# Attention's first tiles over the recurrence's scratch, and the first squares added by VectorE, in a fused FoX / RWKV-7 / memory-attention layer

## The chip, the cores and the metric

The kernel runs on one core of a Trainium2 chip. The metric is the device time of one execution in microseconds; the time of a kernel is the median of its runs.

## The reference

One inference step of one layer, for a prompt of 2048 tokens (width 1024) and for 8 decoding sequences of 16 tokens each, which go through the same projection as 128 further rows. All arithmetic is float32. Cut to what matters here:

```python
h = rms_norm(x, norm_g) @ w_in                        # 1024 -> 3654 columns
fox_cols, rwkv_cols, mem_cols = split(h)
q, k, v, logf, g_f = fox_prep(fox_cols, ...)          # QK-norm, log forget gates
o_f = softmax(q k^T / 8 + c_q - c_k, causal) @ v      # 6 heads x 64, c = cumsum(logf)
xs  = token_shift(rwkv_cols, prev, mu)
o_r, s_new, g_r = rwkv_branch(xs, s0, ...)            # 6 heads x 64, delta-rule state scan
o_m = mem_attend(mq, mk, mv)                          # 4 heads x 64 into 256 memory tokens
o = concat(o_f * silu(g_f), o_r * silu(g_r), o_m * silu(g_m))
y = x + o @ w_out
# rms_norm(x, g) = x * rsqrt(mean(x * x) + eps) * g
```

Outputs are `y` for prompt and samples, the new keys, values and log forgets, the memory's keys and values, the recurrence's last states and the last projected rows.

## The kernel before, in words

Precision is kept by splitting each float32 operand into a high part and the rest (`S.copy` to a rounded type on ScalarE, then a subtraction on VectorE or GpSimd), and by three matmuls: high x high, high x low, low x high. All matmuls go through the helper `mm` (line 59), elementwise operations of two tensors through `tt` (62), with a scalar through `stt` (65) and `ts` (68). So one line of the profile holds many uses, and tiles tell them apart.

**Phase 1** (`p1`) walks over the tokens in four rounds of 512, the first with the 128 sample rows added (640). A round begins with `prep_x`: squares of x, their sums over the 1024 features, `rsqrt` of the mean, x times that norm, split into `xk` (eight tiles). In the first round x comes transposed (features on the partitions), in two groups of 256 and 384 tokens; the squares (`xsq`, line 251, ScalarE) are summed over features by matmuls with a column of ones into `pq`, 128 tokens at a time, one matmul for each feature tile and each 128 tokens. `rsqrt_small` (a scale and add on VectorE, a power on GpSimd) gives `rsq`; a matmul with the identity spreads it (`pb`), and ScalarE copies it to `rb` (269). Later rounds square on ScalarE with an accumulator (261). Then come the LoRA columns (`lora_in`), the columns of the recurrence (`shifted`, `rwkv_in`, `rwkv_mid`, `rwkv_scan`, `rwkv_out`) and the other columns (`wide`, `pair`), as filler between the stages of the recurrence. Projections accumulate in the PSUM tiles `pjd` and `pjt` (pool `pj`). The last round ends with the memory's keys and values (`memory_x`, split tiles `xm` over the recurrence's scratch) and the last states, transposed into `pst` and copied out (937 to 940).

**Phase 2** (`p2`) is attention and the output projection. A unit is a pair of heads and a block of 512 queries. `turned_in` loads tokens into `tok` and transposes them into the PSUM tile `pt`; `split_keys` makes `K1` and `K2`, `queries` makes `Q1` and `Q2`; `fox_max` computes logits (`pm`) and their row maxima on VectorE; `negate` and `rows_` put the negated maxima into `Q1` as an extra row; `attend` computes scores (`pS`), exponentials (`P`, split into `Ph` and `Pl`) and values (`po`), which are copied to `ob`. Memory attention, the samples and the output projection (`out_weights`, `project`, PSUM tile `py` with the tag `pt`) are mixed in between as filler. Weights are loaded as `wr`, split into `W`. `cl` (976 to 983) is the running sum of the samples' cached log forgets.

Memory is handed out by pools, each a stretch of SBUF or PSUM that lies behind the pools opened before it. When phase 1's pools close, phase 2's pools are laid over them, and a tile of phase 2 must wait until all tiles of the phase 1 pools under its pool are done. Before, the order in phase 1 is `c1, rv, sm, rw, xs, ws` in SBUF (constants and state; recurrence tiles; small tiles; recurrence scratch; x; weights) and `pj, pg, ps` in PSUM (3, 2 and 3 banks). In phase 2 it is `lt, c2, kp, wk` in SBUF, which puts `c2` and `kp` over `xs`, and `wk` over `ws`; and `qa` (`pt`, 3 banks), `qb` (`pm`, 2), `qc` (`pS` and `po`, 3) in PSUM, which puts `qa` over `pj` and `qc` over `ps`.

The order of all instructions is not that of the code. `_arrange` collects the whole program, gives every instruction an estimated cost, and runs a list scheduler (`_schedule`) over both phases: on each engine the instruction that can start earliest goes first, ties broken by a rank (`_Problem.emitted`: its place in the program in TensorE's time, less a share of the work that hangs on it). It runs 18 times, with ranks moved between runs towards the middle of the earliest and latest start, and takes the order with the shortest estimate. The order is fixed in the program; each engine, and SyncE's queue of DMA issues, runs its list strictly in that order. What the scheduler knows of overlapping pools is worked out from the tiles' sizes (`_overlaps`).

Of the kernel before, what the change touches and what calls it, by code (L numbers as in the profile page):

```python
# [16 lines left out]
D = 1024  # L17
# [8 lines left out]
PL = "G"  # L26
FILL = 0
WRAW, WHL = 2, 4
# [23 lines left out]
def kernel(ctx: ExitStack, tc: tile.TileContext, I: dict, O: dict):  # L52
# [70 lines left out]
    with ExitStack() as p1:  # L123
        c1 = pools(p1, "c1")

        def c1t(name, shape, dtype=F32):
            return c1.tile(shape, dtype, tag=name, name=name)

        maskG = c1t("maskG", [128, 2, 128], BF16)
        reset = c1t("reset", [128, 640], BF16)  # L130
        bones = c1t("bones", [128, 128], F32R)
# [6 lines left out]
        for dst, src, s1, s2 in ((HW0, V_W0, 0.5, 0.0), (HA0, V_A0, 0.5, 0.0), (NKK, V_KK, -1.0, 0.0),  # L138
                                 (HKK, V_KK, 0.5, 0.0), (HKA, V_KA, 0.5, 0.0), (OHKA, V_KA, -0.5, 1.0),
                                 (GW5, V_GNW, 0.5, 0.0), (GB5, V_GNB, 0.5, 0.0)):  # L140
            ts(V, vh[:, dst:dst + 3], vec[:, src:src + 3], s1, s2, M, A_)
        WUP = c1t("WUP", [96, 2, 384], F32R)
        shp = c1t("shp", [128, 13, 8])
# [4 lines left out]
        V.memset(carry, 0.0)  # L148
        LW = c1t("LW", [96, 2, 640], F32R)
        ST = c1t("ST", [128, 3, 64])  # L150
        V.memset(ST, 0.0)
        AR0 = [c1t(f"AR0_{j}", [128, 2, 512]) for j in range(2)]
        WX = [c1t(f"WX_{j}", [128, 8 * 65]) for j in range(1)]
        XT = [c1t(f"XT_{j}", [128, 8, 64]) for j in range(2)]
        for j in range(2):
# [8 lines left out]

        rv = pools(p1, "rv")
        sm = pools(p1, "sm", bufs=2)
        rw = pools(p1, "rw")
        xs_ = pools(p1, "xs")
        ws = pools(p1, "ws", bufs=WHL)
        pj = pools(p1, "pj", bufs=3, space=bass.MemoryType.PSUM)  # L170
# [51 lines left out]
        def prep_x(tok0, n, xtok, xT, gcol, tiles=None, between=lambda: None):  # L222
# [9 lines left out]
            for t0, t1 in ((0, 2), (2, 5)) if first else ((0, nt),):  # L232
                c0, c1 = 128 * t0, 128 * t1
                if first:
# [14 lines left out]
                    for k in range(KC):  # L249
                        sq = sqs[k // 5 if t0 else 0][:, k % 5 if t0 else k, :]  # L250
                        S.activation(sq, raws[k][:, c0:c1], AF.Square)
                        for t in range(t1 - t0):
                            mm(pq[:, t:t + 1], sq[:, 128 * t:128 * t + 128], one1, start=k + t == 0, stop=k == KC - 1)
                    rsqrt_small(rsq[:, t0:t1], pq[:, 0:t1 - t0], t1 - t0, 1.0 / D, EPS)
# [688 lines left out]
    with ExitStack() as p2:  # L943
        lt = pools(p2, "lt", bufs=2)
        fill = lt.tile([128, FILL], BF16, tag="fill", name="fill", bufs=1) if FILL else None
        c2 = pools(p2, "c2")

        def c2t(name, shape, dtype=F32):
            return c2.tile(shape, dtype, tag=name, name=name)

        kp = pools(p2, "kp")
        wk = pools(p2, "wk", bufs=2)
        qa = pools(p2, "qa", bufs=PTB, space=bass.MemoryType.PSUM)
        qb_ = pools(p2, "qb", bufs=PMB, space=bass.MemoryType.PSUM)
        qc = pools(p2, "qc", space=bass.MemoryType.PSUM)

# [17 lines left out]

        cl = lt.tile([48, 512], F32, tag="P", name="cl", bufs=PB)
        SY.dma_start(cl, I["clf"])
        one48 = lt.tile([48, 512], F32, tag="P", name="one48", bufs=PB)
        V.memset(one48, 1.0)
# [38 lines left out]
        def fox_keys(U, hp):  # L1017

            cs = slice(128 * hp, 128 * hp + 128)
            U["K1"], U["K2"], U["vt"] = [], [], []  # L1020

            def block(g0):
                gs = slice(g0, g0 + 512)
                pt = turned_in(k_d[gs, cs], 512)
                k1 = [kp.tile([128, 512], F32R, tag="K1", name="K1", bufs=2 * NKB) for _ in range(2)]
                k2 = [kp.tile([128, 512], F32R, tag="K2", name="K2", bufs=2 * NKB) for _ in range(2)]
                for h in range(2):
                    split_keys(k1[h], k2[h], pt[64 * h:64 * h + 64], 512)
# [24 lines left out]
        def queries(U, q, qsrc, qb, hp, fox):  # L1053
# [23 lines left out]
            def fox_max(h, t, c0, nk):  # L1077
                n = min(512, nk - c0)
                pm = qb_.tile([128, 512], F32, tag="pm", name="pm", bufs=PMB)
                mm(pm[:, :n], q["Q1"][h][:, 128 * t:128 * t + 128], U["K1"][c0 // 512][h][:, :n])  # L1080
                to = q["mx"][:, h, t, c0 // 512:c0 // 512 + 1]
                if c0 + n == nk:

                    V.tensor_tensor_reduce(out=pm[:, :n], in0=pm[:, :n], in1=mneg[:, 512 - n:], scale=1.0,
                                           scalar=-3.0e38, op0=A_, op1=MAX, accum_out=to)
                else:
                    V.tensor_reduce(out=to, in_=pm[:, :n], op=MAX, axis=AX.X)  # L1087
# [39 lines left out]
        def attend(U, q, qb, hp, fox, gsrc, dst):  # L1127
# [6 lines left out]
            def scores(kt, h):  # L1134
# [5 lines left out]
                if fox and kt >= 4 * qb:  # L1140
                    tt(V, pS[:, c0:c0 + 128], pS[:, c0:c0 + 128], negm[:, 2, :], A_)
                P_ = lt.tile([128, 512], F32, tag="P", name="P", bufs=PB)
                S.activation(P_[:, c0:], pS[:, c0:], AF.Exp, bias=NB[:, qb, 2 * hp + h, kt:kt + 1] if fox else 0.0)  # L1143
                Ph = lt.tile([128, 512], F32R, tag="Ph", name="Ph", bufs=HB)
                Pl = lt.tile([128, 512], F32R, tag="Pl", name="Pl", bufs=LB)
                S.copy(Ph[:, c0:], P_[:, c0:])  # L1146
# [3 lines left out]
            def values(kt, h):  # L1150
# [8 lines left out]
                if kt == last - 1:  # L1159
# [3 lines left out]
                    if h:  # L1163
                        rs = lt.tile([1, 512], F32, tag="rs", name="rs", bufs=1)
                        S.copy(rs, po[h][64:65])
                        S.copy(R["ob"][64:128], po[h][0:64])  # L1166
                    else:

                        S.copy(R["ob"][0:65], po[h][0:65])
                        rs = R["ob"][64:65]  # L1170
# [153 lines left out]
        def out_weights(ks):  # L1324
            W = {}

            def load(k):
                raw = lt.tile([128, D], F32, tag="xo", name="wr")
# [7 lines left out]
        def project(W, ks, t, xsrc, dst):  # L1336
# [3 lines left out]
            def load():  # L1340
                ot = lt.tile([128, 5, 128], F32, tag="ot", name="ot", bufs=1)[:, :n]
                for a, k in enumerate(ks):
                    if a == 0 or k != ks[a - 1] + 1:
                        m = next((b for b in range(a + 1, n) if ks[b] != ks[b - 1] + 1), n) - a
                        SY.dma_start(ot[:, a:a + m], o_d[128 * k:128 * (k + m), ts_].rearrange("(k p) t -> p k t", p=128))
                W["x", t] = xt = lt.tile([128, D], F32, tag="xo", name="xo")
                SY.dma_start(xt, xsrc[ts_, :])
# [133 lines left out]
_TRIES = ((0.3, 0), (0.45, 0), (0.6, 0))  # L1481
_AGAIN = 6
_SHIFT = 0.4
_LOOSE = ("pt", "pj")
# [246 lines left out]
class _Problem:  # L1731
# [306 lines left out]
```

## Time and profile before

| | |
|---|---|
| median of 3 runs | 1809.12 us (1807.52 to 1819.66) |
| profiled execution, its own time | 1797.65 us |
| its span, first to last instruction | 1795.9 us |
| mean granted TensorE clock | 0.972 |
| TensorE busy | 1696.7 us (94%) |
| VectorE, ScalarE, GpSimd busy | 978.1, 897.9, 811.8 us |
| DMA | 303.11 MB, mean 169 GB/s |

The rows of the profile are one execution. A row of the view in order of time has start, length (both in us), engine, line, operation, output and inputs, shape, how many instructions are merged in it, and in brackets how long the engine stood idle before it and what released it. PE is TensorE, DVE VectorE, ACT ScalarE, POOL GpSimd, SPq SyncE's queue of DMA issues. A row of a tile's view has the count, the shortest, median and longest duration in ns, and the first and last start. One float32 matmul shows as two records.

### The profile page before, as it was taken

How to read it: one execution, taken by the hardware profiler on the slowest of the kernel's cores; microseconds unless marked ns; L12 is line 12 of the kernel's file. 1: busy time of each engine (PE TensorE's matmuls, PEld its weight loads, DVE VectorE, ACT ScalarE, POOL GpSimd, SP SyncE). 2: the span in 40 equal slices, each digit the busy share in tenths (PEclk: the TensorE clock that was granted, in tenths of full speed). 3: DMA queues.
4: the chain of work that ended last, by engine and by line, in shares of the span. 5: the costliest groups of instructions: out<-in, count | busy, mean ns of one | idle time of the engine just before them, and what ended most of it. 6: DMA issues, size and time to landing. Idle time of an engine off the chain costs nothing.

```text
span 1795.9 us, 41000 instructions
## 1 busy us (share of the span) xinstructions
PE 1696.7 (94%) x16313; PEld 1362.8 (76%) x16313; DVE 978.1 (54%) x2295; ACT 897.9 (50%) x1783; POOL 811.8 (45%) x824
## 2 busy tenths in 40 slices
PE   7989999999999999999899999799999899999998
PEld 6989989687887788886688887466667666667776
DVE  4654655572454564354574372776745765675214
ACT  5424343523243524233324343588898778886552
POOL 3654543242322242131132151477788566866552
PEclk8999999999999999999999999799999999999999
DMA  6763846653644654644635654534445772444432
GB/s 196 267 202 117 269 144 206 209 178 120 212 156 142 244 184 159 198 155 140 204 109 168 195 160 132 166 121 154 128 149 169 251 251 89 138 142 157 154 111 106
DMA packets 236314, 303.11 MB, mean 169 GB/s; under 512 B 81594, under 2 KB 185976, under 8 KB 220250
## 3 DMA queue, kind: packets, MB, share of 16 engines
q1 hardware_dynamic: 236122, 300.49, 51.5%
q8 instruction: 128, 2.10, 0.5%
q14 instruction: 64, 0.52, 0.1%
HBM read 210.15 MB, written 90.28 MB: 167 GB/s over the span
## 4 chain that ended last, share of the span: by engine, by line
PE 37%; DMA 7%; DVE 7%; ACT 7%; issue 2%; POOL 2%; SPq 1%; DVEq 0%; POOLq 0%; ACTq 0%
PE py L59 8%; PE po L59 6%; PE pjd L59 6%; PE pS L59 5%; PE pjt L59 3%; PE pm L59 2%; ACT P L1143 1%; DMA inv_d<-yt 1%; ACT Ph L1146 1%; POOL Pl L62 1%; DMA sp_d<-spr 1%; DMA xd<-inv_d 1%; DMA rb<-rd 1%; PE pz L59 1%; PE sc L59 1%
## 5 line engine op out<-in xcount | busy, mean ns | idle before, releaser
L59 PE MATMUL pjd<-xk,w 128*128 128x512 f32 (+4 forms) x2280 | 540.2, 378 | 13.0 <-ACT xk L279 4.6
L59 PEld LDWEIGHTS pjd<-xk,w 128*128 128x128 f32 (+1 forms) x2280 | 386.5, 192 | 80.8 <-issue 10.5
L62 POOL TENSOR_TENSOR Pl<-P,Ph 128x512 fp32r<-128x512 f32 (+3 forms) x272 | 318.8, 1183 | 160.6 <-ACT Ph L1146 132.8
L59 PE MATMUL pjt<-w,xk 128*128 128x256 f32 x2040 | 291.4, 290 | 3.9 <-issue 3.9
L59 PEld LDWEIGHTS pjt<-w,xk 128*128 128x128 f32 x2040 | 265.6, 192 | 10.1 <-issue 4.1
L59 PE MATMUL py<-W,oh 128*128 128x512 f32 x816 | 242.6, 399 | 0.9 <-ACT W L1331 0.4
L1143 ACT ACTIVATE P<-pS,NB 128x512 f32<-128x512 f32 x240 | 147.5, 624 | 87.1 <-PE pS L59 34.4
L59 PEld LDWEIGHTS py<-W,oh 128*128 128x128 f32 x816 | 150.9, 189 | 40.1 <-issue 1.0
L59 PE MATMUL pS<-Q,K 128*128 128x512 f32 x480 | 156.6, 387 | 7.1 <-ACT P L1143 4.7
L1146 ACT CAST Ph<-P 128x512 fp32r<-128x512 f32 (+3 forms) x272 | 150.7, 564 | 11.0 <-PE po L59 6.2
L59 PE MATMUL po<-Ph,vt 128*65 128x512 f32 x480 | 153.5, 371 | 2.6 <-ACT ob L1166 1.7
L59 PEld LDWEIGHTS pS<-Q,K 128*128 128x128 f32 x480 | 86.0, 193 | 45.4 <-ACT P L1143 21.6
L1087 DVE TENSOR_REDUCE mx<-pm 128x1 f32<-128x512 f32 x144 | 95.7, 685 | 25.1 <-PE pm L59 23.7
L62 POOL TENSOR_TENSOR nr<-nr,mhalf 128x8 f32<-128x8 f32 (+2 forms) x43 | 62.3, 1448 | 100.3 <-DVE nr L68 87.7
L62 POOL TENSOR_TENSOR w<-wraw,w 128x1024 fp32r<-128x1024 f32 (+1 forms) x34 | 81.6, 2411 | 46.2 <-ACT w L201 33.4
L59 PE MATMUL pm<-K,Q 128*128 128x512 f32 (+2 forms) x240 | 91.2, 399 | 9.2 <-DVE mx L1087 4.0
L59 PE MATMUL po<-Pl,vt 128*65 128x512 f32 x240 | 88.3, 369 | 3.1 <-POOL Pl L62 2.9
L62 DVE TENSOR_TENSOR xo<-py,xo 128x512 f32<-128x512 f32 x68 | 46.2, 685 | 77.9 <-PE py L59 77.6
L59 PEld LDWEIGHTS po<-Ph,vt 128*65 128x65 f32 x480 | 63.4, 136 | 30.9 <-ACT ob L1166 3.3
L62 DVE TENSOR_TENSOR ytmp<-yt 64x14 f32<-64x14 f32 (+9 forms) x210 | 55.0, 262 | 41.8 <-DMA yt<-ld 37.1
L718 ACT COPY qk<-pjt 128x512 f32<-128x512 f32 (+1 forms) x47 | 26.1, 564 | 97.0 <-PE pjt L59 96.7
L59 PEld LDWEIGHTS pm<-K,Q 128*128 128x128 f32 x240 | 46.1, 195 | 31.8 <-DVE mx L1087 11.3
(401 smaller groups left out, 2843.8 us busy)
## 6 DMA issues: line engine op xcount, KB each, us to landing
w<-w_d SPq DMA_DIRECT2D x84, 1024.0 KB
w_d<-w SPq DMA_DIRECT2D x28, 1024.0 KB
y_d<-xo SPq DMA_DIRECT2D x21, 512.0 KB
wraw<-in_w_in SPq DMA_DIRECT2D x36, 256.0 KB
xo<-in_x SPq DMA_DIRECT2D x17, 512.0 KB
xo<-y_d SPq DMA_DIRECT2D x17, 512.0 KB
xt<-in_x SPq DMA_DIRECT2D x24, 256.0 KB
xraw<-in_xT SPq DMA_DIRECT2D x24, 256.0 KB
```

The source lines that it names most:

```text
L59: PE.matmul(out, lhsT, rhs, start=start, stop=stop, skip_group_check=True)
L62: e.tensor_tensor(out=out, in0=a, in1=b, op=op)
L718: S.copy(o_, out)
L1087: V.tensor_reduce(out=to, in_=pm[:, :n], op=MAX, axis=AX.X)
L1143: S.activation(P_[:, c0:], pS[:, c0:], AF.Exp, bias=NB[:, qb, 2 * hp + h, kt:kt + 1] if fox else 0.0)
L1146: S.copy(Ph[:, c0:], P_[:, c0:])
```

## The change

It has four parts.

1. In SBUF, phase 1's order becomes `c1, rv, sm, ce, rw, xs, ws`, where the new pool `ce` takes from `c1` the tiles that only the recurrence's inputs use. In phase 2 `lt` gives five kinds of tile to a new pool `lp`, the first key block of the first pair of heads gets a pool of its own, `k0`, and the order becomes `lt, c2, wk, k0, kp, lp`. A tile `gap` fills `lt` up. `cl` and its ones take the two buffers of `ob`.
2. In PSUM, phase 2's order becomes `qc, qb, qa`. The maxima of the first unit use `pt` tiles.
3. The first 120 nodes of the schedule, counted from the first that uses `c2`, start with a rank that is 60 us earlier.
4. In the first round VectorE adds the eight tiles of squares into the first, and one matmul for each 128 tokens sums over the partitions.

```diff
-FILL = 0
...
     with ExitStack() as p1:
         c1 = pools(p1, "c1")
+        rv = pools(p1, "rv")
+        sm = pools(p1, "sm", bufs=2)
+        ce = pools(p1, "ce")
+        rw = pools(p1, "rw")
+        xs_ = pools(p1, "xs")
+        ws = pools(p1, "ws", bufs=WHL)
...
-        reset = c1t("reset", [128, 640], BF16)
+        reset = c1t("reset", [128, 640], BF16, ce)
-        WUP = c1t("WUP", [96, 2, 384], F32R)
+        WUP = c1t("WUP", [96, 2, 384], F32R, ce)
-        LW = c1t("LW", [96, 2, 640], F32R)
+        LW = c1t("LW", [96, 2, 640], F32R, ce)
-        AR0 = [c1t(f"AR0_{j}", [128, 2, 512]) for j in range(2)]
-        WX = [c1t(f"WX_{j}", [128, 8 * 65]) for j in range(1)]
-        XT = [c1t(f"XT_{j}", [128, 8, 64]) for j in range(2)]
+        AR0 = [c1t(f"AR0_{j}", [128, 2, 512], F32, ce) for j in range(2)]
+        WX = [c1t(f"WX_{j}", [128, 8 * 65], F32, ce) for j in range(1)]
+        XT = [c1t(f"XT_{j}", [128, 8, 64], F32, ce) for j in range(2)]
...
                         S.activation(sq, raws[k][:, c0:c1], AF.Square)
-                        for t in range(t1 - t0):
-                            mm(pq[:, t:t + 1], sq[:, 128 * t:128 * t + 128], one1, start=k + t == 0, stop=k == KC - 1)
+                        if k:
+                            tt(V, sqs[0][:, 0, :], sqs[0][:, 0, :], sq, A_)
+                    for t in range(t1 - t0):
+                        mm(pq[:, t:t + 1], sqs[0][:, 0, 128 * t:128 * t + 128], one1, start=t == 0)
...
         lt = pools(p2, "lt", bufs=2)
         c2 = pools(p2, "c2")
+        wk = pools(p2, "wk", bufs=2)
+        k0 = pools(p2, "k0", bufs=2)
         kp = pools(p2, "kp")
-        wk = pools(p2, "wk", bufs=2)
+        lp = pools(p2, "lp", bufs=2)
+        qc = pools(p2, "qc", space=bass.MemoryType.PSUM)
+        qb_ = pools(p2, "qb", bufs=PMB, space=bass.MemoryType.PSUM)
         qa = pools(p2, "qa", bufs=PTB, space=bass.MemoryType.PSUM)
-        qb_ = pools(p2, "qb", bufs=PMB, space=bass.MemoryType.PSUM)
-        qc = pools(p2, "qc", space=bass.MemoryType.PSUM)
+        gap = lt.tile([128, 112], F32, tag="gap", name="gap", bufs=1)
+        V.memset(gap[0:1, 0:1], 0.0)
...
-        cl = lt.tile([48, 512], F32, tag="P", name="cl", bufs=PB)
+        cl = lt.tile([48, 512], F32, tag="ob", name="cl")
-        one48 = lt.tile([48, 512], F32, tag="P", name="one48", bufs=PB)
+        one48 = lt.tile([48, 512], F32, tag="ob", name="one48")
...
-                k1 = [kp.tile([128, 512], F32R, tag="K1", name="K1", bufs=2 * NKB) for _ in range(2)]
-                k2 = [kp.tile([128, 512], F32R, tag="K2", name="K2", bufs=2 * NKB) for _ in range(2)]
+                at, more = (kp, {"bufs": 2 * NKB}) if hp or g0 else (k0, {})
+                k1 = [at.tile([128, 512], F32R, tag="K1", name="K1", **more) for _ in range(2)]
+                k2 = [at.tile([128, 512], F32R, tag="K2", name="K2", **more) for _ in range(2)]
...
-                pm = qb_.tile([128, 512], F32, tag="pm", name="pm", bufs=PMB)
+                pm = (qb_.tile([128, 512], F32, tag="pm", name="pm", bufs=PMB) if hp or qb else
+                      qa.tile([128, 512], F32, tag="pt", bufs=PTB, name="pm"))
...
# P, Ph, Pl, rs and the raw tiles "xo" (wr, xo): lt.tile(...) becomes lp.tile(...)
...
+_FIRST, _AHEAD = 120, 60000
...
+        first = min(x for x in range(self.count) for n in self.used[x] if self.pool[n].startswith("c2"))
+        for x in range(first, first + _FIRST):
+            rank[x] -= _AHEAD
         return rank
```

More of the change, by code (lines that the diff above doesn't have):

```diff
@@ L124, with c1t @@
         c1 = pools(p1, "c1")
-        def c1t(name, shape, dtype=F32):
-            return c1.tile(shape, dtype, tag=name, name=name)
+        rv = pools(p1, "rv")
[4 more added lines that the diff above has]
+        ws = pools(p1, "ws", bufs=WHL)
+        def c1t(name, shape, dtype=F32, pool=c1):
+            return pool.tile(shape, dtype, tag=name, name=name)
         maskG = c1t("maskG", [128, 2, 128], BF16)
-        reset = c1t("reset", [128, 640], BF16)
+        reset = c1t("reset", [128, 640], BF16, ce)
         bones = c1t("bones", [128, 128], F32R)
@@ L163 @@
         first16 = c1t("first16", [128, 1])
[L165 to L169, printed above, removed]
         pj = pools(p1, "pj", bufs=3, space=bass.MemoryType.PSUM)
@@ L944 @@
         lt = pools(p2, "lt", bufs=2)
-        fill = lt.tile([128, FILL], BF16, tag="fill", name="fill", bufs=1) if FILL else None
         c2 = pools(p2, "c2")
@@ L1141, in scores @@
                     tt(V, pS[:, c0:c0 + 128], pS[:, c0:c0 + 128], negm[:, 2, :], A_)
-                P_ = lt.tile([128, 512], F32, tag="P", name="P", bufs=PB)
+                P_ = lp.tile([128, 512], F32, tag="P", name="P", bufs=PB)
                 S.activation(P_[:, c0:], pS[:, c0:], AF.Exp, bias=NB[:, qb, 2 * hp + h, kt:kt + 1] if fox else 0.0)
-                Ph = lt.tile([128, 512], F32R, tag="Ph", name="Ph", bufs=HB)
-                Pl = lt.tile([128, 512], F32R, tag="Pl", name="Pl", bufs=LB)
+                Ph = lp.tile([128, 512], F32R, tag="Ph", name="Ph", bufs=HB)
+                Pl = lp.tile([128, 512], F32R, tag="Pl", name="Pl", bufs=LB)
                 S.copy(Ph[:, c0:], P_[:, c0:])
@@ L1163, in values @@
                     if h:
-                        rs = lt.tile([1, 512], F32, tag="rs", name="rs", bufs=1)
+                        rs = lp.tile([1, 512], F32, tag="rs", name="rs", bufs=1)
                         S.copy(rs, po[h][64:65])
@@ L1327, in load @@
             def load(k):
-                raw = lt.tile([128, D], F32, tag="xo", name="wr")
+                raw = lp.tile([128, D], F32, tag="xo", name="wr")
                 SY.dma_start(raw, I["w_out"][128 * k:128 * k + 128, :])
@@ L1345, in load @@
                         SY.dma_start(ot[:, a:a + m], o_d[128 * k:128 * (k + m), ts_].rearrange("(k p) t -> p k t", p=128))
-                W["x", t] = xt = lt.tile([128, D], F32, tag="xo", name="xo")
+                W["x", t] = xt = lp.tile([128, D], F32, tag="xo", name="xo")
                 SY.dma_start(xt, xsrc[ts_, :])
```

## The prediction, made before the change was run

> **What bounds the kernel now.** I read the page's busy shares and slices first, to see which engine is full and where it is not.
>
> ```profile
> PE 1696.7 (94%) x16313; PEld 1362.8 (76%) x16313; DVE 978.1 (54%) x2295; ACT 897.9 (50%) x1783; POOL 811.8 (45%) x824
> ```
> ```profile
> PE   7989999999999999999899999799999899999998
> ```
>
> TensorE (PE) is busy 94% of the span. Each slice is 44.9 us, and only two of them fall to 7: slice 0, the start, and slice 25 (1122 to 1167 us), where phase 1 (projections and recurrence) gives way to phase 2 (attention). So I cut the span into stages around both; the columns are the stage, its length, busy time of PE, its weight loads, VectorE (DVE), ScalarE (ACT) and GpSimd (POOL) with counts, granted clock, DMA share and GB/s.
>
> ```profile
> 12.00:24.70 12.70, 11.65 (x53) 11.36 (x54) 8.84 (x24) 6.15 (x18) 5.68 (x7) 1.00 0.66 185
> 24.70:41.00 16.30, 10.11 (x46) 7.94 (x46) 9.55 (x23) 11.20 (x28) 4.54 (x4) 0.79 0.56 183
> 41.00:60.00 19.00, 16.49 (x91) 15.17 (x91) 13.61 (x21) 9.94 (x23) 13.19 (x12) 0.82 0.90 300
> 60.00:1120.00 1060.00, 1013.64 (x12622) 866.25 (x12621) 550.74 (x1366) 381.59 (x809) 350.93 (x354) 0.98 0.54 176
> 1120.00:1130.00 10.00, 10.00 (x89) 7.22 (x87) 1.58 (x5) 3.25 (x7) 1.88 (x2) 1.00 0.14 45
> 1130.00:1138.00 8.00, 4.07 (x19) 3.04 (x17) 5.63 (x11) 1.64 (x4) 5.30 (x9) 0.92 0.56 171
> 1138.00:1160.00 22.00, 16.39 (x48) 10.43 (x49) 18.01 (x44) 15.24 (x27) 6.72 (x13) 0.50 0.67 207
> 1160.00:1175.00 15.00, 12.04 (x49) 7.75 (x48) 14.87 (x36) 12.33 (x27) 11.28 (x15) 0.86 0.41 137
> ```
>
> From 60 to 1120 us PE is busy 1013.64 of 1060 (95.6%) at a clock of 0.98: little to win, and the change does not touch it. At the hand-over, busy time times clock gives PE's work at full speed: 4.07 x 0.92 + 16.39 x 0.50 + 12.04 x 0.86 = 22.3 us in the 45 us from 1130 to 1175. So **22.7 us are lost there**, the most that half of the change could win. In those 45 us VectorE is busy 5.63 + 18.01 + 14.87 = 38.5: it is nearly full while PE is not. Just before, from 1120 to 1130, VectorE has 1.58 of 10 us and the DMA share is 0.14: room that nothing uses.
>
> PE's own rows, in order of time, say what it stood for.
>
> ```profile
> 1129.95 4.13 PE L59 MATMUL pjd<-xk,w 128*128 128x512 f32 x17
> 1138.08 1.11 PE L1004 MATMUL pt<-ident,tok 128*128 128x128 f32 x4 [4.00 <-DVE gth L65]
> ```
> ```profile
> 1159.64 1.11 PE L59 MATMUL po<-Ph,vt 128*65 128x512 f32 x2
> ```
>
> The last projection ends at 1134.08. The first attention transpose (`pt`) starts at 1138.08, released by the VectorE read of the last gate projection: that read empties the `pj` banks, and `pt` lies over them. From there it takes 21.6 us to the first values matmul (`po`).
>
> **The change, part by part.** *PSUM.* `pt` moves from the banks of `pj` to those of `ps`. The last user of `ps` is the transposed final state, copied here:
>
> ```profile
> 1130.40 0.46 ACT L939 COPY sstp<-pst 64x384 f32<-64x384 f32 x1
> ```
>
> So `pt` may start at 1130.86 instead of 1138.08: **7.2 us earlier**, beside the last 3.2 us of projections. The scores and `po` banks move over `pj`, which that same read frees at about 1138.0. They are first needed when keys and queries are split (below: eight casts of 0.58 on ScalarE, 4.6 us), so not before 1135.5, and the maxima follow first. I count this as hidden; if scores wait for it, up to 2 us come back.
>
> *SBUF.* Adding up the tiles' sizes, pool by pool, the constants and loaded tokens (`c2`) and queries (`wk`) now lie over the recurrence's scratch `ce` and `rw`, the first keys (`k0`) over `rw`, instead of over the projection's inputs, which live until 1134.08.
>
> ```profile
> 1112.91 0.69 DVE L62 TENSOR_TENSOR ya<-pa,AR 128x512 f32<-128x512 f32 x1 [2.67 <-PE pa L59]
> ```
> ```profile
> 1117.48 0.72 PE L59 MATMUL pjt<-w,xm 128*128 128x256 f32 x4
> ```
> ```profile
> 1134.11 0.37 SPq L1001 DMA_DIRECT2D tok<-k_d  x1
> ```
>
> `ce` is read last at 1113.6 and `rw` (which holds the memory's `xm`) at 1118.2, so the loads that now issue at 1134.11 can go 16 to 20 us sooner, into the quiet stretch. By themselves they are worth nothing, as `pt` waits longer for its banks; without them the earlier banks would be worth nothing either. The key and query parts follow from 1131: for each of the two, four casts on ScalarE and two subtractions on VectorE, priced by these rows. The bias table `NB` on VectorE (1.32 + 3 x 0.24 = 2.0 us) can leave the crowded stretch altogether.
>
> ```profile
> 1139.23 0.58 ACT L993 CAST K<-pt 64x512 fp32r<-64x512 f32 x1 [0.49 <-PE pt L1004]
> ```
> ```profile
> 1140.32 0.69 DVE L62 TENSOR_TENSOR K<-pt,K 64x512 fp32r<-64x512 f32 x1 [0.86 <-ACT K L994]
> ```
> ```profile
> L62 DVE TENSOR_TENSOR NB<-nck,off x4: 244/245/1322, 1134.5 to 1137.9; 128x96 f32<-128x96 f32 x4
> ```
>
> How much of the 7.2 us survives? What follows is VectorE's: it idles 45 - 38.5 = 6.5 us from 1130 to 1175, and 2.0 of its work can leave, so the ramp cannot end more than about 8.5 us sooner unless work is put off. Floor: if phase 1's own tail (gates, group norm) holds VectorE, about 2. I take **8** for the hand-over: the row nearest is the 7.2, and the output weights' raw tiles, which move to space free at 1134, add a little. Moving `cl` and its ones into the two `ob` buffers delays nothing while the copy-out of `po` comes after the write of `cl`; both are rows of this trace:
>
> ```profile
> L983 SPq DMA_DIRECT2D np_d<-cl x1: 320/320/320, 1156.5 to 1156.5; - x1
> ```
> ```profile
> L1169 ACT COPY ob<-po x2: 572/577/582, 1170.1 to 1190.6; 65x512 f32<-65x512 f32 x2
> ```
>
> 13.6 us of room; at 8 us earlier, 5.6 remain. That cover gone, each us of it is a us of PE. First maxima through three `pt` banks instead of two `pm` banks: nothing to 1 us, and I take nothing, VectorE being their limit.
>
> *First squares.* Now 40 matmuls with one output column sum the squares; then VectorE adds the eight tiles (14 additions in all) and 5 matmuls remain.
>
> ```profile
> 4.57 6.98 PE L59 MATMUL pq<-one,xsq 128*128 128x1 f32 x32 [4.57 <-ACT xsq L251]
> 12.59 1.22 PE L59 MATMUL pb<-ident,rsq 128*128 128x128 f32 x4 [1.04 <-POOL rsq L62]
> 14.27 10.40 PE L59 MATMUL pq<-one,xsq 128*128 128x1 f32 x48 [0.46 <-ACT rb L269]
> ```
> ```profile
> 5.46 1.64 ACT L251 ACTIVATE xsq<-xraw 128x256 f32<-128x256 f32 x5 [0.33 <-DMA xraw<-in_xT]
> ```
> ```profile
> 11.59 0.16 DVE L68 TENSOR_SCALAR rsq<-pq 128x2 f32<-128x2 f32 x1 [10.40 <-PE pq L59]
> 14.25 1.28 DVE L65 SCALAR_TENSOR_TENSOR xraw<-xraw,vec,rb 128x256 f32<-128x256 f32 x3 [2.51 <-ACT rb L269]
> ```
> ```profile
> 34.98 0.55 DVE L62 TENSOR_TENSOR xk<-xraw,xk 128x384 fp32r<-128x384 f32 x1
> ```
>
> Two records are one fp32 matmul, so 0.436 us each. The first group's squares end at 7.10; an addition of 128x256 costs 0.43 (1.28/3), running behind the squares, so the last ends near 8.0; two matmuls end at 8.9. `rsq`, at 11.59 now, comes **2.7 us sooner**. The second group's 24 matmuls hold PE until 24.67. With 7 additions of 0.55 = 3.9 us put into the stage 12 to 24.7, where VectorE has 3.9 us free, its sum is ready between 14 and 18, and PE is free for the projection meanwhile. Each addition waits for its square; queued behind it on VectorE are the multiplies by the norms (14.25), for which ScalarE's casts and then the projection's matmuls wait. But what follows is not only PE: ScalarE copies the second norms only at 31.20, behind a token load.
>
> ```profile
> 30.57 0.63 ACT L261 ACTIVATE xt<-xt 128x512 f32<-128x512 f32 x1 [0.88 <-DMA xt<-in_x]
> ```
> ```profile
> 31.20 0.52 ACT L269 COPY rb<-pb 128x256 f32<-128x256 f32 x2
> ```
>
> Its buffers are those of the constants, which ScalarE casts among the first chain's work, so that load shifts with the first chain, not with the second. So the start wins from -2 (additions stretch VectorE's dense part) to 10 (all of the 16.30 - 10.11 = 6.2 us idle and the low clock behind it); I take **4**, near the 2.7 that the rows give.
>
> **Sum:** 8 + 4 = 12 us. Against the profiled execution's 1797.65 that is 1785.7; the runs' median, 1809.12, lies 11.5 higher than that execution, and against it the forecast is **1797**.
>
> **The rivals.** *Larger (1785).* The planner that orders the list keeps projections back as filler while attention's first tiles are prepared, so PE has work until the first scores, and the start closes its stall: 14 of 22.7 plus 10, 24 us. For it: VectorE and DMA are idle from 1120 to 1130. Against: `pt` cannot precede 1130.9, the recurrence's own chain, and VectorE's 38.5 of 45.
>
> *No gain (1806).* VectorE remains the limit: only `NB`'s 2 us and about 1 at the start are won. For it: 14.87 of 15 us from 1160 to 1175. Beside it stands the clock.
>
> ```profile
> 27.22 2.34 PE L59 MATMUL pjd<-xk,w 128*70 128x256 f32 x17
> 33.74 0.40 PE L59 MATMUL pjd<-xk,w 128*70 128x384 f32 x1 [4.18 <-ACT xk L279]
> ```
>
> PE paused 4.18 us before 33.74, and the clock averaged 0.79 and 0.82 in the stages up to 60. Without the squares' matmuls PE would pause between 9 and about 17, and the lora's first 24 matmuls (17 take 2.34 us on PE, 0.138 each) would take twice as long, 3.3 us, leaving 0.7 of the start's 4.
>
> The Trainium skill, "TensorE: Matmul & The Clock Gate", section "What's actually happening", says that the gate goes to half rate after an idle window of about 3.4 us and needs as long a busy one to return; by that rule alone the time would be about 1800, and the trace agrees with it at 33.74.
>
> *Slower (1818).* The first loads sit in SyncE's one queue, up to 60 us ahead of their old place, and wait there for `ce`. Anything behind them waits too: the weights' reloads, the recurrence's own round trips.
>
> ```profile
> 1094.06 1.06 ACT w L201
> ```
> ```profile
> 1119.27 0.46 SPq L726 DMA_DIRECT2D out_mv_p<-qk  x1
> 1128.80 0.30 SPq L365 DMA_DIRECT2D sp_d<-spr  x1
> ```
>
> The queue is idle for 9.1 us here, so a wait shorter than that, behind 1119.7, is free. Placed before the last weight loads, which the chain that ended last shows in use at 1094, and held until 1113.6, it would stall PE for about 20: net 1797 + 21 = 1818. It decides if the planner's time for `ce` is over 9 us early.
>
> **How the numbers follow.** Forecast (1790 to 1804) 0.52, larger 0.26, no gain 0.15, slower 0.07. One per cent, 18 us, is about what a measurement here can tell from no change: below 1791 is faster, the larger rival and the forecast's edge, 0.31; above 1827 slower, half of that rival, 0.04. The range leaves out the tail of the larger rival and most of the slower one: 1780 to 1810.
>
> **What would show it.** Right: `pt` before 1131 less the start's gain, beside `pjd`; no wait of `pt` on `gth`; token loads before 1120 on that scale; 10 records of `pq` instead of 80, `rsq` near 9 and 18; the clock's dip at the hand-over shorter than 22 us. Wrong: `pt` early but `po` still 21 us after the last projection (VectorE full), or PE waits behind DMA between 1060 and 1120 (the queue), or the projection's first matmuls still beginning at 24 us (the start bound by its loads).

## The result, and the profile after

The changed kernel takes **1789.86 us** (median of 6 runs, 1786.74 to 1797.63), the kernel before, run beside it, 1808.98 (6 runs, 1807.52 to 1819.66): a ratio of **0.9884, 95% interval 0.9859 to 0.9908**, 19.1 us less. The profiled execution took 1788.72 us. The forecast was 1797, in a range of 1780 to 1810.

First the page of the changed kernel: span, busy times and TensorE's 40 slices.

```profile
span 1786.9 us, 40906 instructions
...
PE 1679.5 (94%) x16243; PEld 1347.0 (75%) x16243; DVE 980.2 (55%) x2310; ACT 897.2 (50%) x1783; POOL 808.7 (45%) x824
...
PE   4989999999899999999899999799999999989998
```

The same two slices stand out, and the first has fallen from 7 to 4: TensorE is busy 17.2 us less, of which the 70 records of one-column matmuls that are gone make 70 x 0.217 = 15.2. Then the same stages as before the change, with the same columns (stage, length, busy time of TensorE, its weight loads, VectorE, ScalarE and GpSimd with counts, granted clock, DMA share, GB/s).

```profile
12.00:24.70 12.70, 7.64 (x29) 6.12 (x29) 7.90 (x25) 5.28 (x14) 4.65 (x5) 1.00 0.66 163
24.70:41.00 16.30, 10.21 (x34) 6.41 (x35) 14.60 (x22) 11.95 (x29) 10.51 (x8) 0.94 0.66 215
41.00:60.00 19.00, 17.22 (x101) 15.86 (x101) 12.85 (x29) 10.27 (x25) 7.51 (x8) 0.87 0.98 341
60.00:1120.00 1060.00, 1015.42 (x12693) 869.26 (x12693) 553.39 (x1375) 384.44 (x818) 355.31 (x366) 0.99 0.55 176
1120.00:1130.00 10.00, 7.02 (x36) 4.96 (x34) 4.99 (x10) 7.46 (x14) 4.72 (x11) 0.90 0.73 226
1130.00:1138.00 8.00, 5.49 (x14) 3.24 (x15) 7.83 (x23) 3.19 (x7) 0.26 (x1) 0.50 0.46 143
1138.00:1160.00 22.00, 17.12 (x64) 12.09 (x64) 20.87 (x48) 16.55 (x34) 12.09 (x14) 0.68 0.50 156
1160.00:1175.00 15.00, 14.85 (x79) 10.68 (x77) 11.24 (x25) 13.79 (x28) 8.83 (x11) 1.00 0.48 148
```

Two things are to be seen. From 60 to 1120 us TensorE starts 71 instructions more than before (12693 against 12622): phase 1 runs ahead. At the hand-over VectorE is now the full engine from 1130 to 1160 (28.70 of 30 us), and the dip of the clock has moved forward rather than gone: length times what the clock lacks is 1.0 + 4.0 + 7.0 = 12.0 us from 1120 to 1175, against 0.6 + 11.0 + 2.1 = 13.7 before.

TensorE's rows in order of time (start, length, then as before) show the start and the hand-over of the changed kernel.

```profile
12.09 1.02 PE L58 MATMUL pq<-one,xsq 128*128 128x1 f32 x4 [12.09 <-DVE xsq L61]
...
17.91 1.44 PE L58 MATMUL pq<-one,xsq 128*128 128x1 f32 x6 [2.22 <-ACT rb L272]
...
1121.23 0.27 PE L1012 MATMUL pt<-ident,tok 128*128 128x128 f32 x1
...
1123.67 1.85 PE L58 MATMUL pjd<-xk,w 128*128 128x512 f32 x7
...
1139.07 1.88 PE L58 MATMUL pS<-Q,K 128*128 128x512 f32 x4
...
1142.62 0.45 PE L58 MATMUL po<-Ph,vt 128*65 128x512 f32 x1
```

VectorE's reads of the two sums of squares, in the same view:

```profile
13.15 0.16 DVE L67 TENSOR_SCALAR rsq<-pq 128x2 f32<-128x2 f32 x1
...
19.82 0.15 DVE L67 TENSOR_SCALAR rsq<-pq 128x3 f32<-128x3 f32 x1
```

The first is later than before (11.59), the second 4.9 us sooner (24.71, in before's profile). The first `pt` starts at 1121.23, between projections, with no wait; the last projection ends at 1125.52, and the first `po` comes 17.1 us after it (25.6 before).

One caution on the "before" side: the profiled execution shown there lay 11.5 us under the median. A second profile of the unchanged kernel (the run *before_again* below: 1808.2 us, span 1806.4) is an ordinary one.

```profile
1136.99 4.13 PE L59 MATMUL pjd<-xk,w 128*128 128x512 f32 x17
1145.12 0.66 PE L1004 MATMUL pt<-ident,tok 128*128 128x128 f32 x4 [4.00 <-DVE gth L65]
```

The same instructions in the same order end phase 1 at 1141.12 instead of 1134.08; its first `po` is at 1166.11. Against this execution the spans differ by 19.5 us: the last projection ends 15.6 sooner, from there to the first `po` takes 7.9 less, and from the first `po` to the end takes 4.0 more. So between these two executions **most of the difference is in place before the hand-over begins**.

### The profile page after: what moved, and what is told of

It reads as the page before. It is cut to its first block, busy times and chain, and to the rows that moved or that the text cites. A ratio compares the mean times of both kernels' runs of the same rounds, so it can differ in the third digit from the quotient of the medians.

```text
span 1786.9 us, 40906 instructions
## 1 busy us (share of the span) xinstructions
PE 1679.5 (94%) x16243; PEld 1347.0 (75%) x16243; DVE 980.2 (55%) x2310; ACT 897.2 (50%) x1783; POOL 808.7 (45%) x824
## 4 chain that ended last, share of the span: by engine, by line
PE 51%; DMA 11%; DVE 6%; ACT 5%; POOL 3%; issue 2%; SPq 1%; DVEq 0%; POOLq 0%; ACTq 0%
PE pjd L58 12%; PE py L58 8%; PE po L58 7%; PE pjt L58 6%; PE pS L58 5%; PE pm L58 2%; DMA w<-w_d 1%; DMA xd<-inv_d 1%; POOL Pl L61 1%; PE sc L58 1%; ACT P L1154 1%; PE pz L58 1%; PE pa L58 1%; PE gr L58 1%; DMA AR<-sp_d 1%
## 5 line engine op out<-in xcount | busy, mean ns | idle before, releaser
L58 PE MATMUL pjd<-xk,w 128*128 128x512 f32 (+5 forms) x2280 | 537.8, 377 | 18.7 <-DMA w<-w_d 4.6
L58 PE MATMUL pjt<-w,xk 128*128 128x256 f32 x2040 | 295.5, 291 | 3.0 <-DVE xssg L64 1.7
L58 PE MATMUL pS<-Q,K 128*128 128x512 f32 (+1 forms) x480 | 154.7, 392 | 6.5 <-ACT P L1154 5.3
L58 PE MATMUL pm<-K,Q 128*128 128x512 f32 (+3 forms) x240 | 92.8, 404 | 10.8 <-DVE mx L1095 5.2
```

Of the source, the lines that this page charges most:

```text
L58: PE.matmul(out, lhsT, rhs, start=start, stop=stop, skip_group_check=True)
```

## The experiments

The theories, as the expectations name them. **A**: two separate gains, each of which would be kept alone: the squares at the start, the memory layout at the hand-over. **B**: the hand-over is the whole gain. **C**: what counts is the order that the planner finds for the new program, not the parts as such. **D**: the lead (part 3) makes the hand-over. **E**: VectorE bounds the hand-over, so early transposes are worth next to nothing. All ratios are to the kernel before, run on the same chip beside them. The runs come from several sessions, in which the median of the kernel before lay between 1808.98 and 1811.28; so a difference of 2 us between two runs of different sessions says little.

**1 and 2. The squares alone, and all but the squares.** Both are planned anew.

```diff
 # squares_only: before, with part 4 alone; no_squares: the same lines the other way round, in after (cut)
-  for t in range(t1 - t0): mm(pq[:, t:t + 1], sq[...], one1, ...)          # 40 matmuls
+  if k: tt(V, sqs[0][:, 0, :], sqs[0][:, 0, :], sq, A_)
+  for t in range(t1 - t0): mm(pq[:, t:t + 1], sqs[0][...], one1, ...)      # 5 matmuls
```

> The kernel before with part 4 alone: VectorE adds the first squares, 5 matmuls sum them. Theory A (two separate gains, each kept): the last projection ends some 8 us before the 1134.1 us of before, as in the changed kernel (1125.5), the wait of the first attention transposes on the last gate's read stays (about 4 us), and the time falls by 8 to 10 us of 1809. Theory B (the hand-over is the whole gain): the lead won by the squares is used up by loads within phase 1, the time stays within 3 us. Theory C (the planner's new order, not the parts, makes the differences): any value within 10 us on either side, and the lead does not grow from the start but jumps between stages.

> The changed kernel with part 4 undone: 40 matmuls sum the first squares again; layout, banks and lead stay. Theory A: the last projection ends near 1134, the first values matmul comes about 17 us after the last projection (17.1 in the changed kernel, 25.6 before), and the time is 8 to 10 us above the changed kernel, 1798 to 1800. Theory B: it equals the changed kernel, 1790. Theory C: anything from 1785 to 1805, with phase 1 shifted by amounts that do not start at the squares.

Measured: the squares alone 1795.05 us, 0.9911 (0.9884 to 0.9938); all but the squares 1809.42, 0.9991 (0.9974 to 1.0007). B falls: the layout with its hand-over, planned anew, wins nothing. Taken at their word the two say that the squares are worth 14 to 20 us, where A had 8 to 10 and the prediction gave 10 as the most that the start could win. If the parts simply added up, the two would agree; that they don't points to the order.

**3 and 4. Without the lead, and with the old order of PSUM's pools.**

```diff
-_FIRST, _AHEAD = 120, 60000
+_FIRST, _AHEAD = 120, 0            # no_lead
```
```diff
-        qc ... qb_ ... qa = ...      # after
+        qa ... qb_ ... qc = ...      # old_banks
```

> The changed kernel with the lead of 60 us set to 0; layout, banks and squares stay. If the memory layout alone opens the hand-over (theory A), the planner places the first loads early anyway, since each engine takes what can start first: first transposes still before the last projection ends, first values about 17 us after it, time 1788 to 1793. If the lead is what makes it (theory D), projections go ahead of the first transposes, the first values come 21 us or more after the last projection, and the time is 4 to 8 us above the changed kernel.

> The changed kernel with the PSUM order of before (transposes over the projections' banks, scores over the scan's). Theory A (the banks hold the first transposes): the first transpose again waits for the last gate's read, 3 to 4 us after the last projection, the first values come 21 us or more after the last projection, and the time is 4 to 8 us above the changed kernel, 1794 to 1798. Theory E (VectorE's load after the hand-over is the limit, the early transposes are worth nothing): the first transposes are late as in A, but VectorE is as full and the time is within 2 us of the changed kernel.

Without the lead: 1786.51, 0.9863 (0.9835 to 0.9892), the lowest median of all, though its interval overlaps that of the changed kernel. Its hand-over is as early without the lead: the first `po` starts at 1144.85, 17.2 us after the last projection (1127.66). **D falls.** With the old banks: 1810.59, 1.0006 (0.9983 to 1.0029), the whole gain gone. But this profile already lags at the start, long before any tile of attention exists: the first copy of `spr`, in the recurrence's first round (ScalarE's rows in order of time), and what TensorE waited for between 0 and 70 us beside the first squares (releaser: us in all, times, longest), both of the old banks. The same two waits are 0.8 and 1.6 us in the changed kernel.

```profile
79.85 0.24 ACT L366 COPY spr<-spt 8x128 f32<-8x128 f32 x1
```
```profile
PE pjd L58 <- DVE xsk L64: 5.4, 1, 5.4
PE pjd L58 <- POOL xk L61: 5.2, 2, 4.9
```

The changed kernel has that copy 10.4 us sooner:

```profile
69.42 0.24 ACT L366 COPY spr<-spt 8x128 f32<-8x128 f32 x1
```

The code up to there is the same in both; only the planner's order differs. So 5 to 8 hold the order.

**5. The squares in the old order.** All other instructions keep before's order; the additions stand directly behind what they need.

```diff
+    # squares_only, and in place of the search over plans:
+    at = {i.name: x for i, x in zip(prog[0], _fixed())}      # before's order, written out
```

> The kernel before with VectorE's squares, but with the order of all other instructions held at that of before: no new plan. Its 14 additions stand right behind their squares, its 5 matmuls behind the last addition. Theory A (the squares themselves win the time at the start): the second norms come some 5 us sooner, 4 us or more of that reach the last projection, and the time is 1800 to 1806. Theory C (the 14 us of the run with the squares alone came from the new plan): at most 3 us are won, 1806 to 1812, and the lead is gone by 120 us.

Measured: 1811.35, 1.0002 (0.9978 to 1.0026): nothing. VectorE's rows say why.

```profile
9.62 0.16 DVE L68 TENSOR_SCALAR rsq<-pq 128x2 f32<-128x2 f32 x1 [1.10 <-PE pq L59]
...
23.77 0.15 DVE L68 TENSOR_SCALAR rsq<-pq 128x3 f32<-128x3 f32 x1
```
```profile
15.95 1.44 PE L59 MATMUL pq<-one,xsq 128*128 128x1 f32 x6 [3.87 <-DVE xsq L62]
```

The first norms come 2 us sooner than before, near the 8.9 predicted. The second sum is ready at 17.39, but `rsq` reads it at 23.77: no bracket, VectorE was busy with what stood ahead of it in its list. That chain is only 0.9 us sooner than before's 24.71. The next link loses most of this too: ScalarE, whose list is also that of before, copies the second norms to `rb` behind a token load that it waits for.

```profile
30.35 0.63 ACT L263 ACTIVATE xt<-xt 128x512 f32<-128x512 f32 x1 [1.92 <-DMA xt<-in_x]
...
30.98 0.52 ACT L271 COPY rb<-pb 128x256 f32<-128x256 f32 x2
```

That is 0.2 us sooner than before's 31.20, as the prediction had read that row. In the changed kernel's order the copy comes at 26.43.

**6. The new order without the squares.** After's order held, the 40 matmuls put back behind their squares.

> The changed kernel with the 40 matmuls back, and the order of all other instructions held at that of the changed kernel. Theory A: the 24 matmuls of the second group hold the first projections back by 8 to 10 us, most of it stays, time 1796 to 1800. Theory C: the matmuls cost at most 3 us in the same order, 1790 to 1793, and the 19 us of the newly planned run without the squares were the plan's.

Measured: 1799.46, 0.9949 (0.9929 to 0.9969), 9.6 us over the changed kernel by the medians and 11.8 by the ratios, with intervals that do not touch.

```profile
18.79 10.40 PE L58 MATMUL pq<-one,xsq 128*128 128x1 f32 x48 [3.21 <-ACT rb L270]
```
```profile
29.23 0.16 DVE L67 TENSOR_SCALAR rsq<-pq 128x3 f32<-128x3 f32 x1 [8.45 <-PE pq L58]
```

VectorE idles 8.45 us for the sum, and `rsq` comes at 29.23 where the changed kernel has it at 19.82: 9.4 us later, about the 9.6 of the medians. (The delay does not run through unchanged: in this profile the last projection ends 14.3 us later, at 1139.79, and the span is 10.3 us longer.) So part 4 is worth about 10 us in the order made for it and nothing in the order made without it. Both are ends: neither order was planned for the program that it was put on.

**7 and 8. Old banks, and the old memory layout, with phase 1 in after's order.** Each engine's list of phase 1 is pinned; phase 2 is planned freely.

```diff
+    last = {}
+    for x in _fixed():               # phase 1's nodes in the order of the changed kernel
+        if p.of[x] in last:
+            p.soft[last[p.of[x]]].append(x)
+            p.need[x] += 1
+        last[p.of[x]] = x
```

> The changed kernel with the PSUM order of before, and with phase 1 held on every engine in the order of the changed kernel, so that only the hand-over and phase 2 are planned anew. Theory A (the banks' own worth): last projection near 1125 as in the changed kernel, first transposes 3 to 4 us after it, first values 21 us or more after it, time 4 to 8 us above the changed kernel, 1794 to 1798. Theory C (most of the 21 us of the newly planned run came from phase 1's other order): as A, 1793 to 1798, not 1810. Theory E (banks worth nothing): 1788 to 1792.

> The changed kernel with parts 1 to 3 undone (SBUF, banks, lead), the squares kept, and phase 1 held in the order of the changed kernel. The layout's own worth. Theory A: last projection near 1125, first values 25 us after it as before, time 6 to 9 us above the changed kernel, 1796 to 1799. Theory B (the hand-over is the whole of it): 1805 or more. Theory E (VectorE bounds the hand-over anyway): 1788 to 1793.

Measured: old banks 1790.97, 0.9898 (0.9871 to 0.9924); old layout, that is parts 1 to 3 undone and the squares kept, 1792.05, 0.9906 (0.9877 to 0.9935). The old banks planned freely had taken 1810.59, so **19.6 us hang on the order, not on the banks**: of the 18.7 us between the two profiles' spans 15.2 are in place when the last projection ends (1145.27 against 1130.09), and the rest lies in phase 2, which was planned freely in both. With phase 1's order given the new banks are worth 1.1 us and the layout 2.2 (2.5 and 4.0 by the ratios), neither to be told from nothing; phase 2 was planned anew here too, and may have made up part of a loss. In the pinned profile of the old banks the copy of `spr` and the hand-over read as follows:

```profile
69.58 0.24 ACT L366 COPY spr<-spt 8x128 f32<-8x128 f32 x1
```
```profile
1125.74 4.35 PE L58 MATMUL pjd<-xk,w 128*128 128x512 f32 x18
...
1135.06 1.94 PE L1012 MATMUL pt<-ident,tok 128*128 128x128 f32 x8 [4.96 <-issue]
...
1157.94 0.63 PE L58 MATMUL po<-Ph,vt 128*65 128x512 f32 x1
```

`spr` is back at 69.58. The hand-over is the slow one (`po` 27.9 us after the last projection), yet the whole takes 1.1 us more than the changed kernel.

**9. The layout alone, with phase 1 in before's order.** Parts 1 to 3 without the squares, pinned in the same way.

> Parts 1 to 3 alone (SBUF, banks, lead), no squares by VectorE, and phase 1 held on every engine in the order of the kernel before. The layout's worth under the old order. By the run with the old layout in the changed kernel's order (2 us above the changed kernel), theory E (VectorE bounds the hand-over, the layout is worth about 2 us): 1805 to 1809. Theory A of the prediction (8 us at the hand-over): 1799 to 1803.

Measured: 1806.22, 0.9974 (0.9949 to 1.0000): 5 us, from 0 to 9, where E had 1805 to 1809 and A 1799 to 1803. Its first `po` comes 17.25 us after the last projection, as in the changed kernel.

**10 to 12. The same programs planned anew, and before once more.** Nothing of the work changes: `_STEP` is a constant in the planner's first ranking (how far an instruction of an engine other than TensorE moves the place in the program).

```diff
-_STEP = 100
+_STEP = 101                         # replan_before: of before; replan_after: of after
```

> The kernel before with nothing changed but a constant of the planner (the step of non-TensorE nodes in the first rank, 100 to 101 ns), so that the order is planned anew for the same work. Theory C (plans of equal worth to the planner differ by 10 us or more on the chip): a time outside 1804 to 1814, either way. If plans hardly matter: within 3 us of 1809.

> The changed kernel with the same constant at 101. Theory C: outside 1785 to 1795, and phase 1's lead differs by 5 us or more. If plans hardly matter: 1787 to 1793.

> The kernel before, unchanged, for a profile of a usual execution (the one shown lies 11.5 us below the median of its runs). If executions of this order differ in phase 1, the last projection ends near 1145 instead of 1134.1, and the 25.6 us from there to the first values stay. If they differ in attention, the last projection stays at 1134 and the end is late.

Measured: before replanned **1795.54**, 0.9912 (0.9892 to 0.9933); after replanned 1791.88, 0.9897 (0.9869 to 0.9924); before unchanged 1808.57, 0.9982 (0.9955 to 1.0010). A constant moved by one per cent gives the old kernel 13 to 16 us, as much as the squares alone did. Planned with 101, the two kernels stand at 1791.88 against 1795.54, 3.7 us apart with overlapping intervals. For replan_after C's forecast missed: it had a time outside 1785 to 1795, and 1791.88 is what was forecast if plans hardly matter, although in its profile (of an execution of 1801.43) the last projection ends at 1149.10 instead of 1125.52. The windows of replan_before and of before_again, in that order, show where it comes from.

```profile
0.00:900.00 900.00, 845.12 (x9960) 724.07 (x9960) 473.18 (x1173) 338.83 (x730) 306.30 (x331) 0.98 0.57 185
900.00:1120.00 220.00, 216.38 (x2943) 184.75 (x2942) 109.39 (x272) 76.87 (x163) 71.50 (x61) 1.00 0.50 157
```
```profile
0.00:900.00 900.00, 837.78 (x9930) 719.95 (x9932) 468.75 (x1167) 336.67 (x727) 307.38 (x330) 0.98 0.57 184
900.00:1120.00 220.00, 211.58 (x2814) 180.12 (x2816) 112.34 (x266) 76.96 (x162) 68.90 (x59) 0.98 0.50 157
```

Busy time by clock, TensorE did 7.2 us more work by 900 and 9.0 more from 900 to 1120, in no single place: 16.2 (6.1 and 9.7 in windows of 20 us, in which the rounding of the clock weighs less), near the 14.3 us by which its last projection ends sooner (1126.87 against 1141.12).

**What the hand-over was worth, by TensorE's work.** One stage for each of five profiles, from 5 us before the last projection ends, 50 us long: before, old_layout_pinned, old_banks_pinned, then the two with the new layout, after and layout_old_order.

```profile
1129.10:1179.10 50.00, 37.50 (x148) 25.37 (x147) 41.51 (x94) 32.80 (x64) 24.61 (x37) 0.73 0.53 165
```
```profile
1118.70:1168.70 50.00, 36.94 (x145) 25.30 (x144) 39.48 (x91) 33.78 (x66) 20.77 (x37) 0.73 0.53 168
```
```profile
1125.10:1175.10 50.00, 36.69 (x150) 25.96 (x149) 38.60 (x90) 32.07 (x62) 20.78 (x31) 0.73 0.48 150
```
```profile
1120.50:1170.50 50.00, 39.49 (x160) 27.33 (x159) 41.55 (x94) 36.62 (x71) 23.75 (x34) 0.76 0.52 161
```
```profile
1140.40:1190.40 50.00, 40.93 (x159) 26.97 (x158) 40.16 (x94) 36.11 (x69) 25.62 (x35) 0.76 0.51 156
```

TensorE's busy time by its clock is 27.4, 27.0 and 26.8 us with the old layout or banks, 30.0 and 31.1 with the new: **3 to 4 us** of work won, though the first values come 8 us sooner. VectorE is as full before as after (41.51 and 41.55 of 50, 94 instructions each), and E's ranges were met in 7, 8 and 9. So 1.1 and 2.2 us (7 and 8), 5 (9) and this 3 to 4 agree. That VectorE is what bounds the stage is argued from this, not shown: no run gave it less to do, and the clock, 0.73 to 0.76 in all five, is a rival that no run sets apart.

The same product of busy time and clock, summed over the whole span (in windows of 5 us from 45 us before to 65 us after the end of the last projection, of 10 us elsewhere), divides a profile into work and lost time (the span less that product), roughly, since the recorded clock is rounded and, at the start, doubtful (last section). The 1806.4 us of before_again hold some 1659 us of work and 147 of lost time, the 1786.9 of the changed kernel some 1647 and 140. So **of these 19.5 us about 12 are work that TensorE no longer has, the squares' matmuls (15.2 by their rows), and about 7 are lost time**; in the 110 us around the last projection it loses 20.2 instead of 24.2. With the matmuls put back into the same order (run 6) it is some 1658 and 140. In the old order (run 5) the work is gone as well, but that execution, a long one with 1818.03 us, loses some 167.

What is late next can be read in the changed kernel: VectorE's last read of the `pj` banks, and a weight load of the first scores.

```profile
1138.29 0.67 DVE L64 SCALAR_TENSOR_TENSOR gth<-gth,pjd 128x512 f32<-128x512 f32 x1
```
```profile
1139.51 0.93 PEld L58 LDWEIGHTS pS<-Q,K 128*128 128x128 f32 x3 [0.20 <-ACT Q L1126]
```

The gate's read no longer holds back `pt`, and so VectorE's list puts it 12.8 us behind the last projection. It ends at 1138.96, and the first scores, whose banks now lie over `pj`, start at 1139.07. In four other profiles with the new layout (no_lead, layout_old_order, replan_after, no_squares_same_order) the first scores also start 0.05 to 0.15 us after that read ends, and in a fifth (no_squares) 0.29 us after it. But TensorE has no idle time before them here, and the weight load at 1139.51 waits for ScalarE's cast of the row of maxima, which comes later than the read. So a cost of the new wait is not shown, and that the scores waited for the read is a reading of these times; no run moved the read.

## Why the prediction came out as it did

- **The sum** was 12 us against 19.1, inside the range but nearer the larger rival. Both of its terms were mis-sized, in opposite directions, and a gain of the order's own, which the sum did not have, came on top. That the time fell into the range owes much to luck.
- **Hand-over, 8 us.** The mechanism came as described: `pt` at 1121 beside `pjd`, no wait on `gth`, the first keys' tokens issued at 1102.87, `po` 8 us nearer to the last projection. Its worth was 1 to 5. The failed step is "the ramp cannot end more than about 8.5 us sooner" with the 8 taken close under it: the idle time of VectorE was taken for a gain, and the row nearest (7.2, the earlier `pt`) for its size. The runs show an earlier first tile with VectorE's work in the stage unchanged (41.51 and 41.55 us); TensorE got 3 to 4 us more to do. The prediction's own sign of failure ("`po` still 21 us after the last projection") did not show, so it was no test: `po` came early and the time was not won. The scores' wait for the gate's read, counted as hidden or "up to 2 us", may have come back, but the row of maxima comes 0.55 us after it (1139.51 against 1138.96), so that no cost of it is shown.
- **The start, 4 us.** In the order that the planner made, part 4 is worth about 10 (9.6 by the medians, 11.8 by the ratios), the upper bound of that term. The prediction priced the first group's chain (`rsq` at 8.9); in the changed kernel that chain is later than before (13.15 against 11.59), and the one that is ahead is the second (19.82 against 24.71), whose sum the prediction put between 14 and 18 and which ends at 19.35. It was mis-sized because both chains were laid into before's order, where run 5 confirms that little is to be had: there the load before ScalarE's copy of the norms sets the pace, as the prediction said. The clock's price there, 3.3 us, took all 24 matmuls at 0.138 us, but the first 7 of them already took 0.25 each in the profile of before (1.75 us from 24.54).
- **"From 60 to 1120 us ... little to win, and the change does not touch it."** This is the step that failed most. The change edits no instruction there, but every edit makes the planner order the whole list again. Runs 4 and 7 put 19.6 us on the order, most of it phase 1's, run 10 some 13 to 16 without any edit of the work.
- **The rivals.** *Larger* gave 24 us, 14 of them by a closed stall at the hand-over and 10 at the start; the time lies toward it, and what came is the 10, not the 14. *No gain* named VectorE as the limit of the hand-over, which fits what was measured there, as said above, without being shown. *Slower*: the token loads went out from 1102.87, and their one long issue, 1.36 us, held nothing up: the next issue came only at 1110.21, and the planner put the loads behind the last weight load (1099.65).

As far as the runs take it apart, the 19 us are about 10 from the squares in the new order (run 6), about 8 from that order itself (run 8 has both together: 1809.48 - 1792.05 = 17.4, less 9.6), and about 2 from the layout. A holds for the squares in that order only; **C** explains what the prediction missed: the order's own 8 us, and that the squares pay at all. These parts are differences of medians, good to some 5 us each, and only the squares' part has intervals that do not touch. The two plans tried of each kernel differ by 11 us in their means, near the 12 us of work that is gone. It stays open how good an average plan of either kernel would be, with two plans of each tried, and why executions of one fixed order differ by up to 19 us (before_again: 1798.90 to 1818.21).

## What to carry to other kernels

Where a planner orders the whole program, no edit is local: compare a change with the order held on both sides, and with a second plan of each side, before any microsecond is put down to the edit. A tile that starts 8 us earlier can be worth far less than 8 us, here 1 to 5; compare the bound engine's work in a stage of fixed length, not the time of the first result. Divide the span into that engine's work and its lost time: it tells a removed instruction from a better order. And see where the profiled execution lies among the runs before its milestones are used.

## What the hardware showed that was not expected

The same 17 matmuls of the LoRA columns (128x256) take 2.34 us in the profile of before, 3.11 to 3.26 in four others that have the squares' matmuls ahead of them (before_again, no_squares, layout_old_order, replan_before), and without these, 3.97 in squares_same_order:

```profile
26.22 3.97 PE L59 MATMUL pjd<-xk,w 128*70 128x256 f32 x17
```
```profile
26.22:30.19 3.97, 3.97 (x19) 3.58 (x18) 1.02 (x2) 2.05 (x5) 0.00 (x0) 1.00 0.51 162
```

That is 0.234 us each against 0.138, and yet the recorded clock of that stretch is 1.00. The prediction's clock rival had the slow pace for a TensorE that pauses early. But the 7 such matmuls just ahead, in the profile of before, took 0.25 us each with no pause, right behind 10.40 us of the squares' matmuls, at a recorded clock of 1.00 as well:

```profile
24.54 1.75 PE L59 MATMUL pjd<-xk,w 128*70 128x256 f32 x7
```

So at the very start of a program the record does not explain the pace, and a pause is not needed for it. The loss in squares_same_order is 0.7 to 0.9 us against the four, 1.6 against the fastest. The other surprise is the spread of a program whose order is fixed, about 1% between executions, 1798.90 to 1818.21 in before_again. Its three shortest runs have a mean clock of 0.976 or 0.977, its longest 0.970, but one of 1811.32 has 0.976 and one of 1808.93 has 0.969. The 23 runs of the kernel before in that session lean the same way (0.974 to 0.976 in the three shortest, 0.967 to 0.972 in the three longest); which is cause and which effect is not shown.
